# Condition rows loaded seven half products ahead, their bias fetched with them, and neighbouring weight columns read in one transfer

## The chip, the cores and the metric

The kernel runs on one core of a Trainium2 chip. The metric is the device time of one execution in microseconds; lower is better. The engines named below are TensorE (PE, matmuls), VectorE (DVE), ScalarE (ACT), GpSimd (POOL, here almost only an issuer of DMAs) and SyncE (SP, which issues most loads). Each works through its own list of instructions in order.

## The reference, cut to what matters

```python
sh1, sc1, g1, sh2, sc2, g2 = split(silu(c) @ ada_w + ada_b, 6)     # c: 1 x 1024, ada_w: 1024 x 6144
h = rmsnorm(x, norm1_g) * (1 + sc1) + sh1                          # x: 1024 tokens x 1024
gate_b, gate_c, hv = split(h @ conv_w_in, 3)                       # conv_w_in: 1024 x 3072
y = (gate_b * conv3(gate_c * hv)) @ conv_w_out                     # three taps along 64-token rows
x = x + g1 * y
gate, up = split((rmsnorm(x, norm2_g) * (1 + sc2) + sh2) @ ffn_w_in, 2)
x = x + g2 * ((silu(gate) * up) @ ffn_w_out)                       # d_ff 2816
out = rmsnorm(x, final_g)
```

All is float32. Of the six condition rows, `sh1` and `sc1` are needed at once; `g1`, `sh2`, `sc2` and `g2` only after the first projection. `ada_w` is 24 MB: 4 MB for each of the six rows.

## The kernel before

Every float32 matmul is made as three matmuls of a high and a low part (`TERMS`: high by high, high by low, low by high). The parts come from a split: ACT casts the raw tile to the high part (L83), DVE subtracts to get the low part (L74). The projections further use a two-by-two block scheme with seven products in place of eight (`P1` to `P7`), whose operands are sums of blocks (`AS1` to `AS4` of the activations, `BP3` to `BP7` of the weights, made by DVE subtractions of `wr` tiles at L74).

The part of the program that is changed is the late part of the first projection. Its 24 column tiles of 128 are named by (i, j): i is the tile in a quarter, j is 0, 1 or 2 for `gate_b`, `gate_c` and `hv`. Twelve of them, each with its partner in the other half, are handled in `PAIRS`, two at a time: `Mix(n)` takes `PAIRS[2n:2n+2]`, for n from 0 to 5. A mix needs five products (`PLAN`: P5, P6, P7, P4, P3), and for each of them a left and a right column tile a = 0, 1. Five products times two tiles times six mixes make 60 *half products*; each is 12 matmuls of 128x128 by 128x512 (`product`, L453), into the same PSUM tile `m{n}_{a}` that is emptied and filled anew between products (`after`): after P5, ACT copies it to `z5` (L464) and puts the kept product `p1` in it (L465); after P6, DVE adds to `p1` (L77); after P7, DVE adds `z5` (L77) and multiplies; after P4, the tile is put in its place (ACT copy L490 for j = 2, DVE product L80 else) and refilled with `p1` (L481); after P3, it is put in its place and, for j = 0, the finished gated tile `cv` goes by a POOL DMA to the DRAM tensor `vd` (L486).

A loop `for t in range(62)` sets the order: slot t first issues what was booked with `loads(t, ...)`, then one weight sum, the split for the next product, what was booked with `also(t, ...)`, and then half product t with its `after`. `order5` interleaves mixes 0 and 1 in slots 0 to 19; from slot 20 each mix has ten slots. All this stands under `in_order(SP, DVE, ACT, PE)`, so the four engines execute in the order in which the code is written, whatever is ready. POOL is outside of that list.

Between these products, three of the late condition rows (`g1`, `sh2` and `sc2`, 12 MB of `ada_w`) are computed, nearly without TensorE: `AdaRow` objects `rows[0..5]`, named `ada{j0}_{d0}` (`ada2_0` and `ada2_512` for `g1`; `ada3_0`, `ada3_256`, `ada3_512`, `ada3_768` for `sh2` and `sc2`; 2 MB each). For each, four loads (`load`, L200, SP) bring 512 KB each; ACT scales each by the condition (`scale`, two instructions at L205, and after the second and fourth a POOL DMA that accumulates one tile onto another, L207); DVE adds the rest and splits it (`sums`, L77, and L83/L74); two PE matmuls with ones sum over partitions (L237); then `row` fetches the bias by a POOL DMA (L240), adds it on DVE (L77, tile `ada_b`) for `g1`, or copies on ACT (L243) for the others, and writes the row out (L244). The table `ROWS` holds, for each row, the slots of its loads, of its scales and of its sums; `row` comes two slots after the last sum.

The last slots also load and split `conv_w_out` (`output_load` L937, `output_split`, tiles `wor`, `woh`, `wol`). After the loop come the output products `y` (L1005), whose other operand is `vd` read back (`vl_t`, L993) and split (`vh_t` on ACT, L83).

Of the kernel before, what the change touches and what calls it, by code (L numbers as in the profile page):

```python
# [15 lines left out]
P = 128  # L16
H = 512
# [7 lines left out]
def trunk_kernel(ctx: ExitStack, tc: tile.TileContext, x, c, ada_w, ada_b, norm1_g, norm2_g,  # L25
                 conv_w_in, conv_w, conv_w_out, ffn_w_in, ffn_w_out, final_g, out):
    nc = tc.nc
    x, out = x[0], out[0]
    T, D = x.shape
    KD = D // P  # L30
    KH = KD // 2
# [6 lines left out]
    conv_w_in, conv_w_out, conv_w = conv_w_in[0], conv_w_out[0], conv_w[0]  # L38
# [16 lines left out]
    def t_wop(name, shape):  # L55
        return sb.tile(shape, F32R, name=name, tag="wop", bufs=8)
# [7 lines left out]
    def t2(name, shape=None):  # L64
        return sb.tile(shape or [P, H], F32, name=name, tag="t2", bufs=6)
# [122 lines left out]
    class AdaRow:  # L188
# [32 lines left out]
        def sums_of_rows(self):  # L221
# [7 lines left out]
                    nc.vector.scalar_tensor_tensor(acc, row, by, acc, op0=ALU.mult, op1=ALU.add)  # L229
            self.halves(acc)  # L230

        def row(self, to, bias=False):

            nj = self.nj
            ps = bank(f"{self.name}_ps")
            for i, part in enumerate(self.parts):
                nc.tensor.matmul(ps[0:1, :], lhsT=ones_r, rhs=part, start=i == 0, stop=i == 1)  # L237
            b = t2(f"{self.name}_b")
            if bias:
                nc.gpsimd.dma_start(b[0:1, :], ada_b[0:1, self.j0 * D + self.d0:self.j0 * D + self.d0 + self.w])  # L240
                add(b[0:1, :], ps[0:1, :], b[0:1, :])
            else:
                nc.scalar.copy(b[0:1, :], ps[0:1, :])  # L243
            nc.gpsimd.dma_start(to[:, :, self.d0:self.d0 + self.w], b[0:1, :].rearrange("p (j w) -> p j w", j=nj))  # L244

# [83 lines left out]

    PAIRS = [(0, 2), (0, 1), (1, 2), (1, 1), (0, 0), (2, 2), (2, 1), (1, 0), (3, 2), (3, 1), (2, 0), (3, 0)]
    EARLY = PAIRS[:7]
    place = {(i, j): 3 * j - 2 + i if j else 0 for i, j in EARLY}
    for kp in range(2):
        a_tiles("11", kp), a_tiles("12", kp)
# [2 lines left out]

    aside = dram.tile([len(PAIRS) + 2 * KH, P, H], F32, name="aside")  # L340

# [22 lines left out]
    def save_p1(pair, tile):  # L364
        nc.scalar.copy(tile, xbank[pair])
        nc.gpsimd.dma_start(aside[PAIRS.index(pair)], tile)

    def first_done(pair):

        (i, j), ps = pair, xbank.pop(pair)  # L370
        if j == 1:
            u = parts11.pop(i)
            mul(u, ps, u)
            nc.gpsimd.dma_start(aside[len(PAIRS) + i], u)
        else:
# [4 lines left out]
            else:  # L380
                nc.gpsimd.dma_start(aside[len(PAIRS) + KH + i], u)

# [30 lines left out]
    class Mixes:  # L413
# [5 lines left out]
        def __init__(self, n):  # L419
            self.n, self.pairs, self.raw, self.w, self.ps = n, PAIRS[2 * n:2 * n + 2], {}, {}, {}  # L420

        def load(self, name, tile=t_wraw):

            n = self.n
            if name == "p1":
                self.p1 = t4(f"p1_{n}", [P, 2, H])
                nc.sync.dma_start(self.p1, aside[2 * n:2 * n + 2].rearrange("a p t -> p a t"))
                return
            k0, second = (int(q) - 1 for q in name)
            self.raw[name] = tile(f"wr{name}_{n}", [P, 2, KH, P])  # L430
            for a, (i, j) in enumerate(self.pairs):
                c = j * D + (i + second * KH) * P
                nc.sync.dma_start(self.raw[name][:, a],
                                  conv_w_in[k0 * H:(k0 + 1) * H, c:c + P].rearrange("(k p) n -> p k n", p=P))

        def sum(self, pname):

# [3 lines left out]
                sub(b[o], b[x], b[y])  # L441

        def split(self, pname):
            w = self.w[pname] = [t_wop(f"B{pname}{s}_m{self.n}", [P, 2, KH, P]) for s in "hl"]
            split(*w, self.raw[self.SUMS[pname][0] if pname in self.SUMS else "22"])

        def product(self, q, a):
            (pname, aname), (i, j) = self.PLAN[q], self.pairs[a]
            if q == 0:
                self.ps[a] = bank(f"m{self.n}_{a}")  # L450
            for k in range(KH):
                for n, (wi, hi) in enumerate(TERMS):
                    nc.tensor.matmul(self.ps[a], lhsT=self.w[pname][wi][:, a, k, :],  # L453
                                     rhs=A[aname, k // 2][hi][:, k % 2, :],
                                     start=(q == 0 and k == 0 and n == 0), stop=(k == KH - 1 and n == 2),
                                     skip_group_check=q > 0)
# [205 lines left out]
    with in_order(ENG.SP, ENG.DVE, ENG.Activation, ENG.PE):  # L662
# [5 lines left out]
        more = []  # L668

        def next_loads(k):  # L670

            if k < KD:
                ada.append(Ada(k, 1))
                ada[k].load()
                ada[k].load()
                load0(k)
            elif k == KD:
                xs.extend(Tokens(TH + i) for i in range(TH))
            elif k == KD + 1:
                more.extend(First(pair) for pair in PAIRS[7:9])  # L680
                for m in more:
                    m.load(0)
            elif k == KD + 2:
                more.extend(First(pair) for pair in PAIRS[9:])
                for m in more[2:]:
                    m.load(0)
                for m in more:
                    m.load(1)
# [59 lines left out]
        sub(h_of(0, 0)[1], h0, f(h_of(0, 0)[0]))  # L748
        by_pair = [(pair, range(3)) for pair in EARLY]
        by_term = [(pair, (i,)) for i in (0, 2, 1) for pair in EARLY]  # L750
# [117 lines left out]
        rows = [AdaRow(*p) for p in pieces]  # L868
# [28 lines left out]
        def also(t, *units):  # L897
            ahead[t][1].extend(units)

        def loads(t, *units):  # L900
            ahead[t][0].extend(units)
# [10 lines left out]
        for i, at6 in enumerate((((17, 17, 22), (19, 19, 21)), ((30, 30, 32), (28, 28, 31)),  # L912
                                 ((37, 41, 42), (44, 47, 49)), ((50, 51, 52), (53, 54, 55)))):
            loads(at6[0][0] - 2, conv[i].load)
            for n in range(2):
                for k, t in enumerate(at6[n]):
                    also(t, lambda i=i, n=n, k=k: conv[i].step(n, k))

        ROWS = (((8, 9, 10, 11), (10, 11, 12, 13), (18, 20, 23, 24)),
# [5 lines left out]
        for r, (at_load, at_scale, at_sum) in enumerate(ROWS):  # L925
            for k in range(4):
                loads(at_load[k], lambda r=r, k=k: rows[r].load(t_s if k or r in (0, 3) else t4))
                also(at_scale[k], lambda r=r, k=k: rows[r].scale(k))
                also(at_sum[k], lambda r=r, k=k: rows[r].sums(k))
            if r < 5:  # L930
                also(at_sum[3] + 2, lambda r=r: rows[r].row(rows3) if rows[r].j0 == 3 else rows[r].row(g_rows[0], True))

# [7 lines left out]
        def output_split(k):  # L940
            raw, = wo[k]
            wo[k] = [t_sr(f"wo{s}_{k}", [P, D]) for s in "hl"]
            split(*wo[k], raw)

        for k in range(6):
            loads(52 + k, lambda k=k: output_load(k))
            also(57 + k * 2 // 3, lambda k=k: output_split(k))
        for k in range(6, 8):
            loads(60, lambda k=k: output_load(k))
            also(61, lambda k=k: output_split(k))  # L950
# [2 lines left out]
        for t in range(62):  # L953
# [6 lines left out]
            if t < 60:  # L960
                n, q = order5[t // 2]
# [484 lines left out]
```

## Time and profile before

| | us |
|---|---|
| median of 3 runs (lowest to highest) | 1014.91 (1014.53 to 1016.23) |
| the profiled execution's own time | 1015.26 |
| its span, first to last instruction | 1013.5 |
| PE busy | 988.1 (97%) |
| DVE busy | 716.5 (71%) |
| ACT busy | 484.5 (48%) |
| POOL busy | 101.7 (10%) |

The profile is of one execution. All stages below are in microseconds from the start of its span; the 62 slots begin at 97 us and their last product matmul starts at 276.67 us. PE is busy almost throughout, so what can be won are the few microseconds in which it stands still, and the place to look for them is the list of what PE waited for, stage by stage. Matmul durations are modelled ends: their starts, 0.227 us apart in a row of product matmuls, tell more.

### The profile page before, as it was taken

The numbers are of one execution on the slowest core, as the hardware profiler recorded it, in microseconds if no ns is written. First come the engines' busy times: TensorE is split into PE (matmuls) and PEld (weight loads), VectorE is DVE, ScalarE is ACT, GpSimd is POOL, SyncE is SP. The second block draws the span as 40 slices with busy tenths as digits, with TensorE's granted clock in tenths as the row PEclk, the third lists the DMA queues.
The fourth block names the chain that finished last, engine by engine and source line by source line (L and its number), as shares of the span: only waits on it lengthen the run. The fifth ranks groups of instructions, "written<-read, shape, count | busy, mean of one in ns | idle before, by whom it ended". The sixth has DMA issues, their size and how long they took to land.

```text
span 1013.5 us, 12324 instructions
## 1 busy us (share of the span) xinstructions
PE 988.1 (97%) x4426; PEld 809.8 (80%) x4426; DVE 716.5 (71%) x1037; ACT 484.5 (48%) x767; POOL 101.7 (10%) x183
## 2 busy tenths in 40 slices
PE   8999999989999999999999999999999999999996
PEld 6788887767778878888888888888888888888886
DVE  5767978767846689687756656656656745778885
ACT  6555676665425566333333333333334352544653
POOL 2121001110011110111101101101101110000000
PEclk9999999999999999999999999999999999999999
DMA  9997189988685232265333333333315964578533
GB/s 298 324 329 241 56 247 256 291 252 228 221 255 188 97 110 79 92 192 169 118 100 108 104 98 110 105 94 114 104 32 194 382 224 145 181 249 280 184 127 143
DMA packets 161661, 180.46 MB, mean 178 GB/s; under 512 B 8212, under 2 KB 118912, under 8 KB 161600
## 3 DMA queue, kind: packets, MB, share of 16 engines
q1 hardware_dynamic: 147920, 135.81, 43.3%
q0 software_dynamic: 12448, 40.69, 12.5%
q10 hardware_dynamic: 1232, 3.18, 0.8%
q8 instruction: 34, 0.56, 0.2%
q14 instruction: 27, 0.22, 0.1%
HBM read 135.33 MB, written 38.03 MB: 171 GB/s over the span
## 4 chain that ended last, share of the span: by engine, by line
PE 75%; DMA 8%; DVE 8%; issue 3%; ACT 3%; SPq 1%; POOL 1%; ACTq 0%; POOLq 0%; DVEq 0%
PE X_f L563 23%; PE zP L1375 20%; PE Z_f L563 12%; PE Y_f L563 6%; PE y L1005 5%; PE m L453 3%; DMA ada_w<-in_ada_w_dram 3%; PE x L403 2%; PE x L361 2%; DMA vl_t<-vd 1%; DMA wr<-in_conv_w_in_dram 1%; DMA w0r<-in_conv_w_in_dram 1%; DVE wr L74 1%; DMA vd<-cv 1%; DMA ada_b<-in_ada_b_dram 1%
## 5 line engine op out<-in xcount | busy, mean ns | idle before, releaser
L74 DVE TENSOR_TENSOR BP_f<-wr_f,BP_f 128x512 fp32r<-128x512 f32 x154 | 105.0, 688 | 60.6 <-ACT BP_f L83 58.7
L83 ACT CAST BP_f<-wr_f 128x512 fp32r<-128x512 f32 x154 | 94.2, 621 | 86.1 <-PE Z_f L563 55.8
L1375 PE MATMUL zP<-w3l_P,a3h_P 128*128 128x512 f32 (+1 forms) x319 | 121.8, 382 | 0.0
L1375 PE MATMUL zP<-w3h_P,a3l_P 128*128 128x512 f32 (+1 forms) x319 | 121.7, 382 | 0.0
L1375 PE MATMUL zP<-w3h_P,a3h_P 128*128 128x512 f32 (+1 forms) x319 | 120.4, 382 | 0.6 <-DVE bot L80 0.6
L1375 PEld LDWEIGHTS zP<-w3h_P,a3h_P 128*128 128x128 f32 x319 | 60.0, 188 | 12.5 <-DVE bot L80 0.8
L1375 PEld LDWEIGHTS zP<-w3h_P,a3l_P 128*128 128x128 f32 x319 | 60.0, 188 | 11.6
L1375 PEld LDWEIGHTS zP<-w3l_P,a3h_P 128*128 128x128 f32 x319 | 60.0, 188 | 11.5
L74 DVE TENSOR_TENSOR a3l_P<-a3l_P,a3h_P 128x1024 fp32r<-128x1024 f32 (+1 forms) x42 | 47.3, 1132 | 24.5 <-ACT a3h_P L1230 24.5
L563 PE MATMUL X_f<-A11h,BP_f 128*128 128x512 f32 x176 | 57.7, 390 | 0.0
L563 PE MATMUL X_f<-AS3h,BP_f 128*128 128x512 f32 x176 | 57.6, 389 | 0.0
L563 PE MATMUL Z_f<-AS4h,BP_f 128*128 128x512 f32 x176 | 57.6, 389 | 0.0
L563 PE MATMUL X_f<-AS2h,BP_f 128*128 128x512 f32 x176 | 57.6, 389 | 0.0
L563 PE MATMUL X_f<-A22h,BP_f 128*128 128x512 f32 x176 | 57.6, 389 | 0.0
L563 PE MATMUL Y_f<-A12h,BP_f 128*128 128x512 f32 x176 | 57.5, 389 | 0.0
L563 PE MATMUL Z_f<-AS1h,BP_f 128*128 128x512 f32 x176 | 57.4, 389 | 0.0
L1005 PE MATMUL y<-woh,vh_t 128*128 128x512 f32 x128 | 50.6, 395 | 0.9 <-ACT vh_t L83 0.9
L1005 PE MATMUL y<-woh,vl_t 128*128 128x512 f32 x128 | 50.0, 391 | 0.0
L1005 PE MATMUL y<-wol,vh_t 128*128 128x512 f32 x128 | 49.9, 390 | 0.0
L1230 ACT CAST a3h_P<-a3l_P 128x1024 fp32r<-128x1024 f32 (+1 forms) x42 | 40.7, 979 | 15.2 <-DMA a3l_P<-ad_S 9.0
L74 DVE TENSOR_TENSOR wr_f<-wr_f,wr_f 128x512 f32<-128x512 f32 x66 | 45.3, 689 | 1.5
L77 DVE TENSOR_TENSOR u_f<-Z_f,u_f 128x512 f32<-128x512 f32 x22 | 15.2, 691 | 37.5 <-ACT u_f L580 34.8
(310 smaller groups left out, 2351.4 us busy)
## 6 DMA issues: line engine op xcount, KB each, us to landing
wr_f<-in_ffn_w_in_dram SPq DMA_DIRECT2D x44, 512.0 KB, 4.0
ada_w<-in_ada_w_dram SPq DMA_DIRECT2D x64, 256.0 KB, 6.3
w_P<-in_ffn_w_out_dram SPq DMA_DIRECT2D x30, 512.0 KB, 5.4
wr<-in_conv_w_in_dram SPq DMA_DIRECT2D x48, 256.0 KB, 6.2
a3l_P<-ad_S SPq DMA_DIRECT2D x20, 512.0 KB, 6.2
ad<-a POOLq DMA_DIRECT2D x33, 256.0 KB, 2.4
ada_w<-in_ada_w_dram SPq DMA_DIRECT2D x16, 512.0 KB, 4.0
a3l_P<-ad SPq DMA_DIRECT2D x15, 512.0 KB, 4.0
```

The costliest lines, as they stand in the source:

```text
L74: return nc.vector.tensor_tensor(o, a, b, op=ALU.subtract)
L77: return nc.vector.tensor_tensor(o, a, b, op=ALU.add)
L83: nc.scalar.copy(hi, raw)
L361: nc.tensor.matmul(xbank[pair], lhsT=w0[k][wi][:, place[pair], :], rhs=h_of(k, 0)[hi], start=(k == 0 and i == 0), stop=(k == KD - 1 and i ...
L403: nc.tensor.matmul(xbank[self.pair], lhsT=self.w[wi][:, k, :], rhs=h_of(half * KH + k, 0)[hi], start=(half == 0 and k == 0 and i == 0), st ...
L453: nc.tensor.matmul(self.ps[a], lhsT=self.w[pname][wi][:, a, k, :], rhs=A[aname, k // 2][hi][:, k % 2, :], start=(q == 0 and k == 0 and n = ...
L563: mm = nc.tensor.matmul(ps, lhsT=w[:, wi, 2 * kp + kk, :], rhs=A[aname, kp][hi][:, kk, :], start=(first and kp == 0 and kk == 0 and i == 0 ...
L1005: mm = nc.tensor.matmul(ys[t][n], lhsT=vt[t][vi][:, k, :], rhs=wo[k][wi][:, n * H:(n + 1) * H], start=(k == 0 and i == 0), stop=(k == KD - ...
L1230: nc.scalar.copy(hi, f(lo))
L1375: mm = nc.tensor.matmul((zs[t] if to is None else to)[:, cols], lhsT=a[ai][:, k % 2, t * P:(t + 1) * P], rhs=w[wi][:, k % 2, cols], start= ...
```

## The change

1. `PAIRS` is put in another order so that the two tiles of mix 0 are (0,2) and (1,2), and of mix 1 (0,1) and (1,1): neighbours in `conv_w_in`. The weight tiles are now laid out with the two tiles side by side in a row, and where the two columns are neighbours (mixes 0, 1 and 5) one DMA of 512 KB with rows of 1 KB replaces two of 256 KB with rows of 512 B. That makes 12 weight loads fewer on SP's queue. Before, mix 0 held (0,2), (0,1), and mix 1 held (1,2), (1,1).
2. In `ROWS`, loads stand three to seven slots sooner, and scales one to five; a scale now stands four slots after its load (two of them five), where it stood two to five. The sums of rows 0 to 3 stay, those of rows 4 and 5 move (row 4's first one slot later and its last two sooner, row 5's all sooner by one or two).
3. The bias of the two `g1` rows is fetched by `load_bias` three slots before the last sum, five before it is added; before, it was fetched and added at the same place.
4. The splits of `conv_w_out` stand in slots 57, 58, 59, 60, 61, 61 instead of 57, 57, 58, 59, 59, 60.

```diff
+        bias = None
+        def load_bias(self):
+            self.bias = t2(f"{self.name}_b")
+            nc.gpsimd.dma_start(self.bias[0:1, :], ada_b[0:1, self.j0 * D + self.d0:self.j0 * D + self.d0 + self.w])
+            return self.bias
...
-            b = t2(f"{self.name}_b")
             if bias:
-                nc.gpsimd.dma_start(b[0:1, :], ada_b[0:1, self.j0 * D + self.d0:self.j0 * D + self.d0 + self.w])
+                b = self.bias or self.load_bias()
                 add(b[0:1, :], ps[0:1, :], b[0:1, :])
             else:
+                b = t2(f"{self.name}_b")
                 nc.scalar.copy(b[0:1, :], ps[0:1, :])
...
-    PAIRS = [(0, 2), (0, 1), (1, 2), (1, 1), (0, 0), (2, 2), (2, 1), (1, 0), (3, 2), (3, 1), (2, 0), (3, 0)]
-    EARLY = PAIRS[:7]
+    EARLY = [(0, 2), (0, 1), (1, 2), (1, 1), (0, 0), (2, 2), (2, 1)]
+    LATER = [(1, 0), (3, 2), (3, 1), (2, 0), (3, 0)]
+    PAIRS = [(0, 2), (1, 2), (0, 1), (1, 1)] + EARLY[4:] + LATER
...
-            self.raw[name] = tile(f"wr{name}_{n}", [P, 2, KH, P])
-            for a, (i, j) in enumerate(self.pairs):
-                c = j * D + (i + second * KH) * P
-                nc.sync.dma_start(self.raw[name][:, a],
-                                  conv_w_in[k0 * H:(k0 + 1) * H, c:c + P].rearrange("(k p) n -> p k n", p=P))
+            self.raw[name] = tile(f"wr{name}_{n}", [P, KH, 2 * P])
+            (c0, c1), rows = [j * D + (i + second * KH) * P for i, j in self.pairs], conv_w_in[k0 * H:(k0 + 1) * H, :]
+            for to, c, w in ((0, c0, 2 * P),) if c1 == c0 + P else ((0, c0, P), (P, c1, P)):
+                nc.sync.dma_start(self.raw[name][:, :, to:to + w],
+                                  rows[:, c:c + w].rearrange("(k p) n -> p k n", p=P))
...
-                    nc.tensor.matmul(self.ps[a], lhsT=self.w[pname][wi][:, a, k, :],
+                    nc.tensor.matmul(self.ps[a], lhsT=self.w[pname][wi][:, k, a * P:(a + 1) * P],
...
-        ROWS = (((8, 9, 10, 11), (10, 11, 12, 13), (18, 20, 23, 24)),
-                ((14, 15, 17, 18), (16, 18, 20, 22), (26, 27, 29, 33)),
-                ((22, 23, 24, 25), (24, 25, 26, 28), (34, 37, 38, 39)),
-                ((29, 30, 31, 32), (32, 33, 34, 35), (40, 43, 44, 45)),
-                ((36, 37, 38, 39), (38, 39, 40, 42), (48, 50, 53, 56)),
-                ((43, 44, 45, 46), (45, 46, 47, 48), (57, 58, 59, 60)))
+        ROWS = (((1, 2, 3, 4), (5, 6, 7, 8), (18, 20, 23, 24)),
+                ((10, 11, 12, 13), (14, 15, 16, 17), (26, 27, 29, 33)),
+                ((18, 19, 20, 21), (22, 23, 25, 26), (34, 37, 38, 39)),
+                ((26, 27, 28, 29), (30, 31, 32, 33), (40, 43, 44, 45)),
+                ((33, 34, 35, 36), (37, 38, 39, 40), (49, 50, 51, 53)),
+                ((40, 41, 42, 43), (44, 45, 46, 47), (55, 57, 57, 58)))
...
+            if rows[r].j0 == 2:
+                loads(at_sum[3] - 3, rows[r].load_bias)
...
-            also(57 + k * 2 // 3, lambda k=k: output_split(k))
+            also((57, 58, 59, 60, 61, 61)[k], lambda k=k: output_split(k))
```

What this does to the engines' lists is shown at three places. Lines of the changed kernel are seven to eleven higher for the same statement.

ACT, at the end of the first product of mix 2 (slot 20). `BP7h_m2` is the high part of mix 2's third weight sum, `cv0_1` a convolution's first tap, `z5_2_0` the copy out of the PSUM tile `m2_0`, and the next row its refill. Before:

```order
L205 ACTIVATE ada2_512_w2_1394<-ada2_512_w2_1394,cols_98 128x512 x2
L490 COPY u1_1_1133<-m1_0_1116 128x512
L83 CAST BP7h_m2_1477<-wr12_2_1275 128x1024
L512 ACTIVATE cv0_1_1481<-u0_1_1088,cols2_778 128x1024
L205 ACTIVATE ada2_512_w4_1435<-ada2_512_w4_1435,cols_98 128x512 x2
L464 COPY z5_2_0_1517<-m2_0_1504 128x512
L465 COPY m2_0_1504<-p1_2_1433 128x512
```

And with the change:

```order
L83 CAST BP6h_m2_1436<-wr11_2_1277 128x1024
L521 ACTIVATE cv0_0_1440<-u0_0_1079,cols2_778 128x1024
L205 ACTIVATE ada2_512_w6_1348<-ada2_512_w6_1348,cols_98 128x512 x2
L499 COPY u1_1_1106<-m0_1_1089 128x512
L83 CAST BP7h_m2_1480<-wr12_2_1280 128x1024
L521 ACTIVATE cv0_1_1484<-u0_1_1080,cols2_778 128x1024
L473 COPY z5_2_0_1521<-m2_0_1508 128x512
L474 COPY m2_0_1508<-p1_2_1434 128x512
```

The scales of `ada2_512` that stood around the convolution's tap and right ahead of the copy of `z5_2_0` are now all ahead of `u1_1`, and nothing but the tap stands between `BP7h_m2` and the copy.

POOL, around the bias of the row `ada2_512` (the DMA from `in_ada_b_dram`, L240 before and L236 now). Rows with L207 accumulate one tile of a condition row onto another, `vd` rows send a finished `cv` tile away, and the `g1_row` row sends the biased row. Before:

```order
L486 DMA vd_125<-cv0_0_1441 128x1024
L207 DMA ada3_0_w4_1592<-ada3_0_w6_1616 128x1024
L486 DMA vd_125<-cv0_1_1481 128x1024
L207 DMA ada3_256_w0_1712<-ada3_256_w2_1736 128x1024
L240 DMA ada2_512_b_1860<-in_ada_b_dram 1x16x32
L207 DMA ada3_256_w4_1762<-ada3_256_w6_1786 128x1024
L244 DMA g1_row_126<-ada2_512_b_1860 16x1x32
```

And with the change:

```order
L251 DMA g1_row_126<-ada2_0_b_1527 16x1x32
L495 DMA vd_125<-cv0_0_1440 128x1024
L236 DMA ada2_512_b_1737<-in_ada_b_dram 1x16x32
L495 DMA vd_125<-cv0_1_1484 128x1024
L207 DMA ada3_256_w0_1638<-ada3_256_w2_1665 128x1024
L207 DMA ada3_256_w4_1691<-ada3_256_w6_1713 128x1024
L251 DMA g1_row_126<-ada2_512_b_1737 16x1x32
```

The bias fetch stood behind the first accumulation of `ada3_256`; it now stands ahead of it, and ahead of `cv0_1` too.

DVE, at the end of the loop. `cv3_1` multiplied by `m5_1` is the last step of the last mix; `wol` rows are the low parts of `conv_w_out`, `vl_t` rows those of `vd` read back. Before:

```order
L74 TENSOR_TENSOR wol_2_2377<-wor_2_2290,woh_2_2376 128x1024
L80 TENSOR_TENSOR cv2_1_2079<-m5_0_2214,cv2_1_2079 128x512
L77 TENSOR_TENSOR ada3_768_w0_2054<-ada3_768_w0_2054 128x512
L74 TENSOR_TENSOR wol_3_2397<-wor_3_2307,woh_3_2396 128x1024
L74 TENSOR_TENSOR wol_4_2401<-wor_4_2324,woh_4_2400 128x1024
L80 TENSOR_TENSOR cv3_1_2274<-m5_1_2235,cv3_1_2274 128x512
L74 TENSOR_TENSOR ada3_768_l_2424<-ada3_768_w0_2054,ada3_768_h_2423 128x512
L74 TENSOR_TENSOR wol_5_2428<-wor_5_2344,woh_5_2427 128x1024
L74 TENSOR_TENSOR wol_6_2432<-wor_6_2419,woh_6_2431 128x1024
L74 TENSOR_TENSOR wol_7_2436<-wor_7_2421,woh_7_2435 128x1024
```

And with the change:

```order
L74 TENSOR_TENSOR wol_1_2366<-wor_1_2257,woh_1_2365 128x1024
L80 TENSOR_TENSOR cv2_1_2073<-m5_0_2202,cv2_1_2073 128x512
L74 TENSOR_TENSOR wol_2_2385<-wor_2_2282,woh_2_2384 128x1024
L80 TENSOR_TENSOR cv3_1_2263<-m5_1_2224,cv3_1_2263 128x512
L74 TENSOR_TENSOR wol_3_2408<-wor_3_2299,woh_3_2407 128x1024
L74 TENSOR_TENSOR wol_4_2412<-wor_4_2323,woh_4_2411 128x1024
L74 TENSOR_TENSOR wol_5_2416<-wor_5_2339,woh_5_2415 128x1024
L74 TENSOR_TENSOR wol_6_2420<-wor_6_2403,woh_6_2419 128x1024
L74 TENSOR_TENSOR wol_7_2424<-wor_7_2405,woh_7_2423 128x1024
L74 TENSOR_TENSOR vl_t2_2506<-vl_t2_2506,vh_t2_2505 128x512
```

The product of `cv3_1` stood behind `wol_3` and `wol_4` and now stands ahead of both; the low part `vl_t2` went behind all `wol` rows, and row `ada3_768` has left this stretch.

More of the change, by code (lines that the diff above doesn't have):

```diff
@@ L443, in split @@
         def split(self, pname):
-            w = self.w[pname] = [t_wop(f"B{pname}{s}_m{self.n}", [P, 2, KH, P]) for s in "hl"]
+            w = self.w[pname] = [t_wop(f"B{pname}{s}_m{self.n}", [P, KH, 2 * P]) for s in "hl"]
             split(*w, self.raw[self.SUMS[pname][0] if pname in self.SUMS else "22"])
@@ L679, in next_loads @@
             elif k == KD + 1:
-                more.extend(First(pair) for pair in PAIRS[7:9])
+                more.extend(First(pair) for pair in LATER[:2])
                 for m in more:
@@ L683, in next_loads @@
             elif k == KD + 2:
-                more.extend(First(pair) for pair in PAIRS[9:])
+                more.extend(First(pair) for pair in LATER[2:])
                 for m in more[2:]:
```

## The prediction

> **What bounds the kernel now.** I read the page's totals first, then the busy times by stage, then what PE waited for in the stage that the change touches, and then the timeline of each engine around each of those waits.
>
> ```profile
> span 1013.5 us, 12324 instructions
> PE 988.1 (97%) x4426; PEld 809.8 (80%) x4426; DVE 716.5 (71%) x1037; ACT 484.5 (48%) x767; POOL 101.7 (10%) x183
> 97.00:300.00 203.00, 193.20 (x831) 154.42 (x830) 157.80 (x176) 118.62 (x163) 20.73 (x31) 0.99 0.80 231
> 300.00:1013.00 713.00, 703.96 (x3164) 582.93 (x3162) 492.55 (x728) 306.23 (x493) 60.88 (x106) 1.00 0.45 147
> ```
>
> The second pair of rows counts PE first: busy time and, in brackets, instructions. PE is the bound. From 97 to 300 us, which is the 62 slots and the first output products, it is idle for 203.00 - 193.20 = 9.8 us, as much as in the 713 us behind (9.0). What it waits for there:
>
> ```profile
> PE m L453 <- DVE z L77: 3.7, 1, 3.7
> PE m L453 <- ACT m L481: 2.8, 2, 1.6
> PE m L453 <- ACT m L465: 1.3, 1, 1.3
> PE m L453 <- DVE p L77: 1.1, 2, 0.8
> PE y L1005 <- ACT vh_t L83: 0.9, 1, 0.9
> ```
>
> These five groups, seven waits, are the whole 9.8 us. They cost more than their idle time. In a row of product matmuls starts are 0.227 us apart, and after a wait the first few come slower:
>
> ```profile
> 201.82 0.39 PE L453 MATMUL m<-A22l,BP4h_m 128*128 128x512 f32 x1
> 202.05 0.39 PE L453 MATMUL m<-A22h,BP4l_m 128*128 128x512 f32 x1
> 206.09 0.79 PE L453 MATMUL m<-A22h,BP4h_m 128*128 128x512 f32 x1 [3.66 <-DVE z L77]
> 206.69 0.63 PE L453 MATMUL m<-A22l,BP4h_m 128*128 128x512 f32 x1
> 209.49 0.40 PE L453 MATMUL m<-A22h,BP4l_m 128*128 128x512 f32 x1
> ```
>
> From 206.09 to 209.49 nine starts take 3.40 us where 9 x 0.227 = 2.04 would do. So this wait (C below) costs 3.66 idle and 1.4 to 1.6 of slowed matmuls. I summed, for all 831 PE rows, what each start-to-start distance over 0.33 us has above 0.227: 14.2 us in all, of which 5.4 are C. That is the most that the change can win here; the profiled execution's own time is 1015.26, and the median of the runs lies 0.35 below it. A difference of 0.2%, 2 us, is about what a measurement of this kernel can tell.
>
> **The seven waits, and what the change does to each.** I give idle time, and with the slow first starts in brackets.
>
> A, 1.31 (1.8), slot 22: P6 of mix 2 waits for the ACT copy that refills `m2_0`.
>
> ```profile
> 156.30 1.32 ACT L205 ACTIVATE ada_w<-ada_w,cols 128x512 f32<-128x512 f32 x2
> 157.53 0.56 ACT L464 COPY z<-m 128x512 f32<-128x512 f32 x1
> 158.12 0.59 ACT L465 COPY m<-p 128x512 f32<-128x512 f32 x1
> 158.76 0.50 PE L453 MATMUL m<-AS2h,BP6h_m 128*128 128x512 f32 x1 [1.31 <-ACT m L465]
> ```
>
> The two scales of `ada2_512` stand ahead of the copies. In the new ACT list they are earlier, and the P5 tile that the copies need was done a whole half product (12 x 0.227 = 2.7 us) before PE stood still. The copies, 1.2 us for the pair, then wait for PE alone. A goes.
>
> C, 3.66 (5.4), slot 37: the second tile of P4 of mix 3 needs a DVE sum that stands behind the bias sum.
>
> ```profile
> 196.63 0.80 POOL L240 DMA_DIRECT2D ada_b<-in_ada_b_dram  x1
> 204.76 0.68 DVE L77 TENSOR_TENSOR ada_b<-ada_ps,ada_b 1x512 f32<-1x512 f32 x1 [3.53 <-DMA ada_b<-in_ada_b_dram]
> 205.37 0.67 DVE L77 TENSOR_TENSOR z<-m,z 128x512 f32<-128x512 f32 x1
> DMA to landing us min/median/max: 1.7/5.2/9.2
> ```
>
> The bias DMA was issued at 196.63 and landed 8.06 us later; 9.2 is the longest of the four. With the change it is booked five slots ahead, 5 x 12 x 0.227 = 13.6 us before the add, and its place in POOL's list is behind a `vd` DMA whose `cv0_0` is ready at slot 26. So it lands at least 4 us before it is wanted, and C loses its 5.4. What is late next is DVE itself: its list up to that sum is done 0 to 0.3 us after PE wants it. Two slots on, at 39, the refill of `m3_1` stands in a chain of a multiplication, two copies, a cast and two DVE passes, which C had hidden; with durations from their rows I get 0.45 late. Cost of both: 0.6.
>
> E, 1.62 (1.9), slot 49, and F, 1.22 (1.5), slot 59: refills of `m4_1` and `m5_1`.
>
> ```profile
> 235.73 1.34 ACT L205 ACTIVATE ada_w<-ada_w,cols 128x512 f32<-128x512 f32 x2 [2.46 <-DMA ada_w<-in_ada_w_dram]
> 243.00 0.69 DVE L80 TENSOR_TENSOR u<-m,u 128x512 f32<-128x512 f32 x1
> 243.72 0.59 ACT L481 COPY m<-p 128x512 f32<-128x512 f32 x1 [1.36 <-DVE u L80]
> 272.87 0.62 ACT L83 CAST vh_t<-vl_t 128x512 fp32r<-128x512 f32 x1 [3.16 <-DMA vl_t<-vd]
> 273.39 0.58 ACT L481 COPY m<-p 128x512 f32<-128x512 f32 x1
> ```
>
> E begins with ACT idle for 2.46 us until a load of `ada3_768` lands, which pushes the cast of `BP6h` and all behind it. That load is now three slots (8 us) earlier and its scale one slot. F's refill stands behind the cast of `vh_t2`, which waits for a `vd` read; now the refill is ahead of it, and one `wol` pass (2.36 for two, 1.2 for one) leaves the DVE list ahead of it. I take 0.3 each for what DVE's queue still costs (0 if its passes run at the rows' times from here, 1.9 and 1.5 if nothing moves).
>
> B, 0.78 (1.05), and D, 0.31 (0.6), slots 24 and 44: P7 waits for the DVE add to `p1`.
>
> ```profile
> 161.78 2.44 DVE L516 SCALAR_TENSOR_TENSOR cv<-u,cols,cv 128x1008 f32<-128x1008 f32 x2
> 164.25 0.69 DVE L80 TENSOR_TENSOR cv<-cv,gate 128x512 f32<-128x512 f32 x1
> 164.86 0.68 DVE L77 TENSOR_TENSOR p<-m,z 128x512 f32<-128x512 f32 x1
> 227.46 0.68 DVE L77 TENSOR_TENSOR p<-m,z 128x512 f32<-128x512 f32 x1
> ```
>
> Here DVE's queue is simply long: two convolution taps (2.44) and two more passes stand ahead of the add at 164.86. The amount of DVE work stays. For B the copies of A come sooner and start the queue sooner: 0.3 left, between 0 and 1.05. D began with a scale that waited for its load; I put it at 0.
>
> G, 0.90 (1.45), at 294: `y` waits for the last `vd` read back.
>
> ```profile
> 276.60 0.69 DVE L80 TENSOR_TENSOR cv<-m,cv 128x512 f32<-128x512 f32 x1
> 277.80 2.35 DVE L74 TENSOR_TENSOR wol<-wor,woh 128x1024 fp32r<-128x1024 f32 x2
> 280.07 0.69 DVE L80 TENSOR_TENSOR cv<-m,cv 128x512 f32<-128x512 f32 x1
> 281.06 0.53 POOL L486 DMA_DIRECT2D vd<-cv  x1 [1.20 <-DVE cv L80]
> 293.66 0.62 ACT L83 CAST vh_t<-vl_t 128x512 fp32r<-128x512 f32 x1 [9.58 <-DMA vl_t<-vd]
> 294.33 0.50 PE L1005 MATMUL y<-woh,vh_t 128*128 128x512 f32 x1 [0.90 <-ACT vh_t L83]
> ```
>
> The last product matmul starts at 276.67, yet the multiplication runs only at 280.07, behind two `wol` passes of 1.2 us; then POOL's DMA, the read and the cast take 280.07 to 294.28. With the change two passes of `wol` and one of `ada3_768` are behind the multiplication and `g1` is behind the `vd` DMA on POOL: the chain starts 1.2 us or more sooner. Two `y` matmuls that PE ran ahead of the last product now come after it, so PE also arrives 0.45 later. G goes, with 0.1 left.
>
> **What the change adds.** Scales now run earlier and their tiles are reused earlier. The tightest place I find is slot 34: in ACT's new list the convolution's tap on `cv1_1` reuses the buffer of an `ada3_0` tile, so it waits for the accumulating DMA of that row, and the cast for `BP7` of mix 3 stands behind it, then three DVE passes and the add to `p1` that PE wants.
>
> ```profile
> L207 POOL DMA_DIRECT2D ada_w<-ada_w x12: 851/875/914, 131.9 to 245.9; - x12
> DMA to landing us min/median/max: 4.6/7.9/9.6
> ```
>
> The scale before it runs at about 170.2 in old times; with 7.9 us to landing the tap starts at 178.4, and the add is done about 0.6 us after PE wants it. With 4.6 the wait is 0; with 9.6 it is 2.3. I take 1.0, since this sum follows some fifteen passes by their mean durations and since a late DVE pass already ends three of the seven waits. Slots 28 and 54 come out at 0 to 0.2 and 0 to 0.5: 0.35 for both.
>
> Twelve weight loads fewer are twelve issues of about 0.4 us fewer on SP. By the loop's bookings a load stands one to three products ahead of its use, so this is worth nothing on the path; nor do I charge the 1 KB rows anything, since DVE needs both column tiles in one pass and waits for the later of the two loads anyway. If a merged load landed as late as the slower of two does now, nothing changes. The first row's four loads move up to slots 1 to 4 and its scales to 5 to 8, where DVE is full:
>
> ```profile
> 110.00:130.00 20.00, 20.00 (x90) 16.57 (x89) 19.97 (x22) 9.81 (x11) 0.00 (x0) 1.00 0.29 79
> ```
>
> The third number is DVE: 19.97 of 20 us busy. PE does not wait there now, so what is late by less than its lead costs nothing. ACT waits for DVE between its casts, the scales fit into those gaps, and the casts that come about 1.4 us later (one scale pair) are ones that DVE takes up later than that: 0 for the early row, with up to 1.5 if one of them is not. The last split slots cost nothing but what G counts. Behind 300 us nothing moves.
>
> **Sum.** Left of the 14.2: A 0, B 0.3, C and slot 39 0.75, D 0, E 0.3, F 0.3, G 0.1, slot 34 1.0, slots 28 and 54 0.35, small slow starts that belong to none of them 0.5: 3.6. The saving is 10.6; 1015.26 - 10.6 = 1004.7, and with the 0.35 between this execution and the median, 1004.3.
>
> **Rivals.** (1) The queues take the waits back. DVE and ACT do the same work in the same time, so B, D, E and F return in full at neighbouring slots (5.0) and slot 34 costs 2.0. For it: DVE at 19.97 of 20, and three of the seven waits end on a late DVE pass. Against it: E and F begin with ACT waiting for DMAs that are now early. The saving is then A 1.8, C 5.4 less 0.75, G 1.45, less 2.0: 5.9, or 1009.0. (2) All new waits stay out: the saving is 14.2 - 0.5 = 13.7, or 1001.2. For it: each new wait is at most 0.5 us by my passes but slot 34's. (3) The bias comes no sooner because POOL's list holds it behind something that waits: C stays, 10.6 - 4.65 = 6.0, or 1009.0. Against it: the `vd` DMA ahead of it needs only `cv0_0`. (4) C's slowed matmuls were of the profiled execution only. The runs shown differ by 1.7 us, about the size of what the slowed starts cost, so some executions may not have had them. C then had 3.9 to give (3.66 and 0.2), the saving is 9.1, and with it 1005.8. Against it: the profiled execution, which had them, lies in the middle of the three. [...] (5) Slower: the tap on `cv1_1` at slot 34. Each microsecond that the accumulating DMA lands later goes to PE in full, since ACT, DVE and PE stand in order behind it. It decides when that wait passes 1.0 + 10.6 = 11.6 us, that is, when the accumulation lands at about 189 in old times; over 2 us more, and it is slower beyond doubt: 1017 at 13.6. For it: the tile's accumulation is issued behind another on POOL, which waits for its own loads and scales first. Against it: 9.6 us is the longest landing seen, and the table issues these loads four and five slots earlier than before.
>
> **How the numbers follow.** My forecast 0.48; rival 1 0.22; rival 2 0.13; rival 4 0.07; rival 3 0.03; slower by over 0.2%, rival 5 above all, 0.04; a mix in which so much returns that it is within 0.2% 0.03. The range goes from rival 2, 1001.2, to a little over rivals 1 and 3, 1009.5; outside of it lie the last two cases and the edges of rivals 1 and 2, some 0.15. The forecast's own bounds, with each term at its ends, are about 1002.5 to 1006.5. Faster is 0.93, within 0.2% 0.03, slower 0.04.
>
> **What would show it.** In the list of PE's waits the 3.7 behind DVE `z` is gone, or under 0.5, and no matmul after it is slowed; the wait for the refill at L465 is gone; the two at L481 are under 0.5 each; `y` no longer waits for `vh_t`. The bias DMA is issued some 14 us before its add. PE's idle time from 97 to 300 is 2 to 4 us in place of 9.8. A wait of over 1.5 us at slot 34, with ACT behind a POOL DMA, would show that I took the accumulation too lightly; waits behind `p` or `z` passes of DVE at many slots would show rival 1; a lasting wait before 157 would mean that the early row disturbs the first two mixes.

## The result and the profile after

The changed kernel takes 1002.46 us (median of 4, 1000.76 to 1002.73) against 1014.81 (median of 4, one execution more than in the table of before): the ratio is 0.987, 95% interval 0.986 to 0.989. The profiled execution took 1002.73. Its page totals, and the busy times of two stretches, as before with PE first:

```profile
span 1000.9 us, 12305 instructions
PE 983.8 (98%) x4426; PEld 808.9 (81%) x4426; DVE 716.3 (72%) x1037; ACT 484.2 (48%) x767; POOL 101.0 (10%) x183
20.00:40.00 20.00, 18.23 (x83) 14.48 (x83) 15.88 (x39) 7.86 (x11) 0.11 (x1) 0.91 1.17 308
98.00:288.00 190.00, 189.96 (x835) 154.81 (x834) 158.46 (x178) 118.73 (x163) 20.71 (x31) 1.00 0.84 244
```

From 98 to 288 us, which holds the 62 slots and the first `y` products, PE is busy 189.96 of 190.00 us. In place of seven waits with 9.8 us the list of PE's waits is empty for that stage. Counted in matmul starts (what lies above 0.227 us between starts more than 0.33 apart), the stage loses 0.58 us where it lost 14.2. The third row shows the granted clock, third from the end of the row: 0.91 from 20 to 40 us, where it was 1.00 before. There some of the gain went back in this execution, 0.9 us until the loop began; the second profile of the same kernel has starts 0.23 us apart at 33 us (below).

C, slot 37, in the timelines of POOL, DVE and PE:

```profile
174.05 0.50 POOL L236 DMA_DIRECT2D ada_b<-in_ada_b_dram  x1
196.99 0.67 DVE L77 TENSOR_TENSOR ada_b<-ada_ps,ada_b 1x512 f32<-1x512 f32 x1
197.59 0.67 DVE L77 TENSOR_TENSOR z<-m,z 128x512 f32<-128x512 f32 x1
200.00 0.39 PE L462 MATMUL m<-A22h,BP4h_m 128*128 128x512 f32 x1
```

The bias DMA goes out at 174.05, 23 us ahead of the add, where the forecast said some 14: POOL is outside the list that `in_order` holds and runs ahead of the slots (PE begins slot 30, for which this DMA is booked, at 180.46). The add at 196.99 waits for nothing. The sum that PE wants is done at 198.26, 1.7 us before PE takes it up at 200.00. A and G:

```profile
155.67 0.59 ACT L473 COPY z<-m 128x512 f32<-128x512 f32 x1 [2.27 <-PE m L462]
156.29 0.59 ACT L474 COPY m<-p 128x512 f32<-128x512 f32 x1
265.24 1.22 DVE L74 TENSOR_TENSOR wol<-wor,woh 128x1024 fp32r<-128x1024 f32 x1
266.38 0.68 DVE L80 TENSOR_TENSOR cv<-m,cv 128x512 f32<-128x512 f32 x1
267.36 0.53 POOL L495 DMA_DIRECT2D vd<-cv  x1 [1.20 <-DVE cv L80]
278.51 0.62 ACT L83 CAST vh_t<-vl_t 128x512 fp32r<-128x512 f32 x1 [3.83 <-DMA vl_t<-vd]
```

The copy into `z5` now waits for PE, and the refill is done at 156.88, 1.3 us before P6 starts at 158.19. At the end of the loop one `wol` pass instead of two stands between the last product and the multiplication, and the cast of `vh_t` is done before PE comes to it.

### The profile page after: what moved, and what is told of

It is laid out like the page before. It is cut to its first block, busy times and chain, and to the rows that moved or that the text cites. A ratio compares the mean times of both kernels' runs of the same rounds, so it can differ in the third digit from the quotient of the medians.

```text
span 1000.9 us, 12305 instructions
## 1 busy us (share of the span) xinstructions
PE 983.8 (98%) x4426; PEld 808.9 (81%) x4426; DVE 716.3 (72%) x1037; ACT 484.2 (48%) x767; POOL 101.0 (10%) x183
## 2 busy tenths in 40 slices
DMA packets 155325, 180.46 MB, mean 180 GB/s; under 512 B 8020, under 2 KB 112576, under 8 KB 155264
## 4 chain that ended last, share of the span: by engine, by line
PE 91%; DMA 3%; DVE 2%; SPq 2%; ACT 1%; issue 1%; POOL 0%; POOLq 0%; ACTq 0%; DVEq 0%
PE X_f L572 23%; PE zP L1386 20%; PE m L462 16%; PE Z_f L572 12%; PE y L1016 7%; PE Y_f L572 6%; PE x L412 3%; PE x L370 2%; SPq L154 1%; DMA ada_w<-in_ada_w_dram 1%; PE x1T L989 1%; SPq L354 1%; DMA wr_f<-in_ffn_w_in_dram 1%; DMA x<-in_x_dram 0%; DMA vl_t<-vd 0%
```

## The experiments

Two theories went in. P: each of the seven waits hangs on one instruction in a wrong place, so that parts of the change act alone. Q: the gain comes of fewer and earlier loads as a whole. "Stage loss" is the sum over starts, as above, for 205 us from the first product of the loop, in the profiled execution alone. Each ratio is to executions of the kernel before that were taken beside it; their medians lie between 1014.81 and 1015.78.

| kernel | median us | ratio to before (95%) | stage loss us |
|---|---|---|---|
| before | 1014.81 | 1 | 14.23 |
| changed | 1002.46 | 0.9872 (0.9855 to 0.9889) | 0.58 |
| bias alone, on before | 1011.28 | 0.9967 (0.9956 to 0.9978) | 10.01 |
| changed, late bias | 1004.14 | 0.9902 (0.9886 to 0.9917) | 2.32 |
| changed, old table of rows | 1007.91 | 0.9936 (0.9922 to 0.9950) | 8.05 |
| changed, two loads for each merged one | 1001.38 | 0.9867 (0.9850 to 0.9885) | 1.02 |
| changed, old pairs and two loads | 1001.60 | 0.9868 (0.9850 to 0.9886) | 1.41 |
| changed, old end | 1004.50 | 0.9898 (0.9882 to 0.9914) | 3.59 |
| changed, early loads but old scale slots | 1009.07 | 0.9941 (0.9925 to 0.9956) | 9.02 |
| the same, `ada3_0` with new scale slots | 1003.14 | 0.9875 (0.9857 to 0.9893) | 2.01 |
| changed, one ACT tap five times | 1004.57 | 0.9887 (0.9869 to 0.9906) | 2.87 |
| changed, terms reordered at 30 us | 1002.56 | 0.9876 (0.9859 to 0.9894) | 0.59 |
| changed, once more | 1001.98 | 0.9867 (0.9846 to 0.9888) | 0.58 |

**The bias alone.** The kernel before with this edit, and the method `load_bias` that it calls:

```diff
+            if rows[r].j0 == 2:
+                loads(at_sum[3] - 3, rows[r].load_bias)
```

> The kernel before with the early bias fetch alone. Theory P (each of the seven waits hangs on one instruction that stood in a wrong place): wait C (3.66 idle, 5.4 with slowed matmuls) goes, its successor at slot 39 costs 0.4 to 1, the other six waits stay with 6.1 us idle; time 4.5 to 5 below the kernel before, about 1010. Theory Q (the gain comes from the whole, fewer and earlier loads, which relieve the DMA queues and with them DVE and ACT): the bias lands early but DVE is late anyway, C shrinks only in part, 1012 or more.

```profile
PE m L460 <- ACT m L488: 4.1, 3, 1.6
PE m L460 <- DVE p L77: 1.1, 2, 0.8
PE y L1014 <- ACT vh_t L83: 1.0, 1, 1.0
PE m L460 <- ACT m L472: 0.9, 1, 0.9
```

C is gone from PE's waits, the other six are there (the group of refills at L488 now has three). The third is C's successor, the refill of `m3_1` at slot 39: 1.05 us idle, where 0.4 to 1 was expected. The loss falls by 4.2 us, the median by 3.9, from 1015.13. The time lies between the two expectations; the waits are those of P.

**The changed kernel with the late bias,** the two lines above taken out of it.

> The changed kernel with the bias fetched where it is added, as before. Theory P: in POOL's list the fetch now stands behind the second accumulation of ada3_256 at 192, so it lands at 196 to 201 where DVE takes it up at 197; PE waits 0 to 2.5 us at slot 37, time 1002.5 to 1005. If the bias cost what it cost before the change, a wait of 3.7 with slowed matmuls would come back: 1007 to 1008. Theory Q: with the queues relieved the fetch lands in 2 to 4 us, no wait, 1002.5.

```profile
PE m L462 <- ACT m L490: 1.0, 1, 1.0
192.70 0.84 POOL L236 DMA_DIRECT2D ada_b<-in_ada_b_dram  x1
198.90 0.68 DVE L77 TENSOR_TENSOR ada_b<-ada_ps,ada_b 1x512 f32<-1x512 f32 x1 [1.86 <-DMA ada_b<-in_ada_b_dram]
```

The bias lands 1.86 us late, and of that PE pays 0.12 at slot 37, 0.07 at 38 and 1.05 at 39 (the row above; waits that short are not listed). So the early bias is worth 4.2 us on the kernel before and 1.7 here. With the early rows the late fetch is issued 3.9 us sooner (192.70 against 196.63) while PE is 2.3 us further along, and it lands after 6.1 us in place of 8.06, in both kernels within 0.5 us of the accumulating DMA issued just ahead of it. The parts are not independent in this pair.

**The old table of rows in the changed kernel.**

```diff
-        ROWS = (((1, 2, 3, 4), (5, 6, 7, 8), (18, 20, 23, 24)),
+        ROWS = (((8, 9, 10, 11), (10, 11, 12, 13), (18, 20, 23, 24)),
...
```

> The changed kernel with the old table of rows (loads, scales and sums), but early bias, merged loads and new slots for the last splits. Theory P: A, B, D and E return (5.3 us with slow starts), F and G in part since the sums of the last row stand at 57 to 60 again (1 to 2), C stays away: 1008 to 1009.5. Theory Q: most of the gain stays with the merged loads, under 1006.

```profile
PE m L462 <- ACT m L490: 2.2, 2, 1.1
PE m L462 <- ACT m L474: 2.1, 1, 2.1
PE m L462 <- DVE p L77: 1.2, 2, 0.8
PE m L462 <- DVE z L77: 0.5, 1, 0.5
136.95 1.34 ACT L205 ACTIVATE ada_w<-ada_w,cols 128x512 f32<-128x512 f32 x2 [2.56 <-DMA ada_w<-in_ada_w_dram]
```

By the new table the loads of the first row stand seven slots sooner, those of the others three to five; an old scale stood two to four slots after its load. A (L474, 2.1), B and D (`p`, 1.2 in two) and E (1.1, one of the two refills at L490) are back. So is C's successor at slot 39 (1.05, the other), and DVE is 0.5 us late at slot 37 (`z`), though the bias is early; neither was expected. F and G stay away, although the old sums of the last row are back too. 7.5 us of loss are back, the most of the four parts of the change. The last row shows where A begins: ACT waits 2.56 us for a load of `ada2_0`, 20 us ahead of the wait on PE. The run with early loads and old scale slots (below) has the same ACT list here without that wait. Counted from the start of the loop, ACT is 2.6 us later than there at this row and still 2.7 us later at the copy into `z5`.

**Two loads for each merged one, and the old pairs too.**

```diff
-            for to, c, w in ((0, c0, 2 * P),) if c1 == c0 + P else ((0, c0, P), (P, c1, P)):
+            for to, c, w in ((0, c0, P), (P, c1, P)):
```

> The changed kernel with two loads of 256 KB in place of each merged one; order of pairs and all else as changed. Theory P: no wait comes back, within 0.3 us of the changed kernel, 1002.5. Theory Q: twelve more issues on SP and rows of 512 B make weights late, 1 us or more slower, with waits of ACT and DVE on wr tiles.

> The changed kernel with the old order of pairs and two loads everywhere; rows, bias and last slots as changed. Theory P: no wait comes back that costs over 0.3 us, 1002.5 within 0.5. Theory Q: 1 us or more slower.

Stage losses of 1.02 and 1.41 against 0.58: one wait on `z` of 0.16 us in the first, and waits of 0.15 on `p` and 0.13 on `z` in the second. The medians are 1001.38 and 1001.60, not above the changed kernel's 1001.98 to 1002.46. Twelve DMAs fewer and rows of 1 KB for 512 B are worth less than these runs can tell. Of Q, the half that speaks of fewer loads has nothing left for it.

**The old end.**

```diff
-            also((57, 58, 59, 60, 61, 61)[k], lambda k=k: output_split(k))
+            also(57 + k * 2 // 3, lambda k=k: output_split(k))
```

and the old sums of rows 4 and 5.

> The changed kernel with the old slots at the end: splits of conv_w_out at 57, 57, 58, 59, 59, 60 and the old sums of rows 4 and 5; loads and scales as changed. Theory P: F and G return, 1.5 and 1.45 with their slow starts, 1004.5 to 1005.5, with PE waits for the refill at slot 59 and for vh_t. Rival: F and G came only from the waits ahead of them (E pushed them), so they stay away: under 1003.2.

```profile
PE m L462 <- ACT m L490: 1.5, 1, 1.5
PE y L1016 <- ACT vh_t L83: 0.7, 1, 0.7
263.58 0.62 ACT L83 CAST vh_t<-vl_t 128x512 fp32r<-128x512 f32 x1 [3.30 <-DMA vl_t<-vd]
264.10 0.58 ACT L490 COPY m<-p 128x512 f32<-128x512 f32 x1
```

F and G return, as F was in the kernel before: the refill at 264.10 right behind a cast that waited 3.30 us for `vd`. Together 3.0 us of loss, 2 to 2.5 in the medians. With the old rows but the new end they stayed away, so the old sums alone do not bring them back: it takes the old slots of the splits. Whether those slots would do it with the new sums, no run shows.

**Early loads, old scale slots.**

```diff
-                ((18, 19, 20, 21), (22, 23, 25, 26), (34, 37, 38, 39)),
+                ((18, 19, 20, 21), (24, 25, 26, 28), (34, 37, 38, 39)),
...
```

and the old scale slots in the five other rows.

> The changed kernel with the early loads but each scale in its old slot. If A and E came from where the scale stands in ACT's list, A returns at 1.3 idle and with it B (0.8), and E in part: 1004.5 to 1006. If they came from scales that waited for their loads (1.62 us at 147 and 2.46 at 235 in the kernel before), early loads alone remove them: under 1003.2, with A under 0.4.

```profile
PE m L462 <- ACT m L474: 4.1, 1, 4.1
PE m L462 <- DVE p L77: 0.9, 2, 0.7
180.44 0.89 POOL L207 DMA_DIRECT2D ada_w<-ada_w  x1 [4.82 <-ACT ada_w L205]
155.05 1.32 ACT L205 ACTIVATE ada_w<-ada_w,cols 128x512 f32<-128x512 f32 x2
156.28 0.56 ACT L473 COPY z<-m 128x512 f32<-128x512 f32 x1
188.62 1.15 ACT L521 ACTIVATE cv<-u,cols 128x1024 f32<-128x1024 f32 x1 [6.61 <-DMA ada_w<-ada_w]
190.92 0.80 PE L462 MATMUL m<-AS2h,BP6h_m 128*128 128x512 f32 x1 [4.09 <-ACT m L474]
191.51 0.63 PE L462 MATMUL m<-AS2l,BP6h_m 128*128 128x512 f32 x1
196.63 0.49 PE L462 MATMUL m<-AS2l,BP6h_m 128*128 128x512 f32 x1
```

Neither expectation had this. A and E are gone: the scales stand right ahead of the copy of `z5` again (155.05 and 156.28), and PE finds the refill done 0.5 us early. So A and E came from scales that waited for loads. B is there (0.7 at slot 24). But a new wait of 4.1 us stands at slot 32: the tap on `cv1_0` is to write into a buffer that the accumulating DMA of `ada3_0` still reads, waits 6.61 us for it (issued 180.44, landed 188.54), and the refill of `m3_0` is behind it on ACT. After the wait the matmuls start 0.43 apart for 5.7 us. The prediction had named the tap on `cv1_1`; here that one starts at 177.76, ahead of the DMA, and the next tap inherits the delay.

**The same with new scale slots for `ada3_0` alone.**

> The kernel with early loads and old scale slots, except that row ada3_0 has its new scale slots. If the wait of 4.1 us at slot 32 there came from the tap on cv1_0, whose buffer waited for ada3_0's late accumulating DMA (180.44 to 188.54), it is gone together with its slowed matmuls, and what is left is the wait on p in slot 24 (0.7) and slot 54 (0.2): 1003 to 1004. If the old scales crowd ACT in general, half of the wait stays: 1005 or more.

The 4.1 us wait and the slowed matmuls are gone. In the list of PE's waits only the row for `p` is left, the same as above (0.7 at slot 24, 0.2 at slot 54), and the time is 1003.14 us. That is the first expectation, and it shows that one late accumulation cost 7 us of stage loss.

**A late ACT by itself.**

```diff
-                nc.scalar.mul(self.cv[n], mixed[i, n], cw[1])
+                for _ in range(5 if (i, n) == (1, 1) else 1):
+                    nc.scalar.mul(self.cv[n], mixed[i, n], cw[1])
```

> The price of lateness on ACT just ahead of slot 34, by itself: the changed kernel with the first tap of cv1_1 executed five times in place of once (same result each time), 4.2 to 4.6 us more on ACT ahead of the cast for BP7 of mix 3. If each microsecond there goes to PE in full beyond a lead of about 1.1 us, as the prediction had it, PE loses 3.1 us or more, 1005.5 or more. If idle stretches of ACT and DVE behind it give back some (DVE waits 2.0 us at 183.6, ACT 2.8 us at 169.9 and 1.8 at 178.9 in the profile of the changed kernel), the loss is about 1.5, half at the refill of m3_0 in slot 32 and half at p in slot 34: 1004.

```profile
PE m L462 <- ACT m L474: 1.4, 2, 1.0
PE m L462 <- ACT m L490: 0.4, 1, 0.4
174.70 5.89 ACT L522 ACTIVATE cv<-u,cols 128x1024 f32<-128x1024 f32 x5
180.63 1.27 DVE L526 SCALAR_TENSOR_TENSOR cv<-u,cols,cv 128x1008 f32<-128x1008 f32 x1 [4.50 <-ACT cv L522]
190.72 0.68 DVE L77 TENSOR_TENSOR p<-m,z 128x512 f32<-128x512 f32 x1
```

The five taps take 5.89 us where one took 1.15, DVE idles 4.50 us for them, and PE loses 2.3 us of stage loss, between the two expectations. So idle stretches did give back about half. (The expectation put one of them, on ACT at 169.9, at 2.8 us; in the trace it is 3.3.) The place was right for slot 32 alone: 1.0 there and 0.35 at slot 33, both refills on ACT, and 0.4 at slot 39. There is none at slot 34, where the add on `p` is done at 191.40, in time.

**A faster version, tried.** `for n, (pair, terms) in enumerate(by_term if k < 3 else by_pair)` in the first projection; a second line of the edit keeps the sum of the next condition row behind as many matmuls as before.

> A try at a faster version: the changed kernel, and in the first part of the program (row block 2 of the first projection, at 29 us) the terms that need the low part of the activations come last, as they do for row block 1, so that PE has 14 matmuls to do while DVE makes that part. The wait of 0.92 us at 30 (1.2 with its slow start) goes: 1001.3. If the slowed matmuls that follow that wait in the profiled execution of the changed kernel (9 starts at 0.43, 1.7 us) come from it, they go too in every execution: about 1000, with a mean clock of 0.998 throughout. If they come by chance, independent of that wait, some executions keep 0.996.

```profile
33.95 0.38 PE L179 MATMUL ada_ps<-ones,ada_acc 128*128 128x1 f32 x2 [1.29 <-DVE ada_acc L77]
```

The wait for `A11l` is gone, and 1.29 us of waiting for `ada_acc` came in its place 3 us later, since the same DVE list makes both. 1002.56 us: no gain. The mean clock of its four executions is 0.996, not 0.998: in its profile the slowed matmuls stand at 17 to 20 us instead of 33 (granted clock 0.72 from 15 to 20 us, 0.94 from 20 to 25 and 1.00 from 30 to 40), so they do not hang on that wait alone. None of these runs beats the changed kernel by more than they can tell.

**The changed kernel once more.**

> The changed kernel once more, beside executions of the kernel before on the same chip. If the slowed matmuls follow a long wait by chance, the kernel before spreads over 4 us or more from run to run and the changed kernel, which has no long wait but the one at 30 us, over 2.5 at most; median about 1002.

1001.98 us, 1001.33 to 1002.82. The seven executions of the kernel before on that chip go from 1013.94 to 1018.26. Both spreads are as expected. The PE timeline at the same instructions, of the first profile of the changed kernel and then of this one:

```profile
33.03 0.60 PE L370 MATMUL x<-A11h,w0h 128*128 128x512 f32 x1
33.43 0.63 PE L370 MATMUL x<-A11l,w0h 128*128 128x512 f32 x1
36.42 0.51 PE L370 MATMUL x<-A11h,w0l 128*128 128x512 f32 x1
```

```profile
33.45 0.48 PE L370 MATMUL x<-A11h,w0h 128*128 128x512 f32 x1
33.77 0.39 PE L370 MATMUL x<-A11l,w0h 128*128 128x512 f32 x1
35.38 0.40 PE L370 MATMUL x<-A11h,w0l 128*128 128x512 f32 x1
```

From the first to the last of these rows, eight steps, one takes 3.39 us and the other 1.93; the waits ahead of them are the same (0.92 for `A11l`, three smaller).

## Why the prediction was right, step by step

1004.3 us was forecast, with 1001.2 to 1009.5, and 1002.46 came. The saving in the stage was 13.65 us where the sum said 10.6; so in this stage rival 2, with 13.7, is what happened. Of the 3.6 us that the sum left over, 0.58 came, 0.30 at slot 39 and 0.27 at slot 49. That the time is nearer to the forecast than the stage is chance: the 0.9 us lost ahead of the loop in the profiled execution hide part of the difference.

- C: right in mechanism, and its successor at slot 39 was right in place. (Between 206.09 and 209.49 lie eight steps, not nine, so the slowed matmuls cost 1.6; and the working ends at 0.6 for both places, while the sum takes 0.75.) DVE's list was said to end 0 to 0.3 late at slot 37; it has 1.7 us to spare. The refill at slot 39 was said to be 0.45 late and costs 0.04 idle, 0.3 with slow starts. Three other runs show it at 1.05 idle: the early bias alone, the late bias, and the old table of rows.
- A: gone, but the step's reason failed. It was put down to the two scales ahead of `z5`. With the scales there and the loads early, PE does not wait; with the old table ACT waits 2.56 us for a load, and A is back. In the kernel before, ACT waits for loads 1.04 us at 134 and 1.62 us at 147, both ahead of A. The scales passed on a lateness that began at a load.
- E: right, and for the reason given (the load of `ada3_768`). B and D: gone with slack of 0.8 and 1.2 us; B was given 0.3. B is the one that needs early scales too: it is there at 0.7 in both runs with early loads and old scale slots.
- F and G: right; they came back with the old slots of the splits and the old sums, and not with the old sums alone. F has 0.16 us of slack, G's cast is 2 us or more ahead.
- Merged loads at nothing: right, by two runs.
- Slot 34, the largest term left (1.0) and the slower rival: the term was mis-sized. Its working began with 7.9 us from issue to landing of the accumulating DMA, the median of the kernel before. Measured:

```profile
170.18 0.86 POOL L207 DMA_DIRECT2D ada_w<-ada_w  x1 [5.95 <-ACT ada_w L205]
176.36 1.15 ACT L521 ACTIVATE cv<-u,cols 128x1024 f32<-128x1024 f32 x1
185.62 1.22 DVE L74 TENSOR_TENSOR BP4l_m<-wr,BP4h_m 128x1024 fp32r<-128x1024 f32 x1 [2.00 <-ACT BP4h_m L83]
189.85 0.69 DVE L77 TENSOR_TENSOR p<-m,z 128x512 f32<-128x512 f32 x1
191.34 0.39 PE L462 MATMUL m<-AS3h,BP7h_m 128*128 128x512 f32 x1
DMA to landing us min/median/max: 4.6/6.0/9.6
DMA to landing us min/median/max: 4.7/8.3/9.5
```

The DMA landed at 176.16, 6.0 us after its issue, just before ACT came to the tap; DVE then has an idle gap of 2.00 us, which the forecast's passes had not, and `p` is done 0.8 us before PE. The last two rows are the accumulating DMAs of the changed kernel and of the one with old rows: the median landing falls from 8.3 to 6.0 by the table of rows alone (6.0 and 6.1 without merged loads). With early loads and old scale slots it is 8.2, so it goes with the slots of the scales, which issue these DMAs, and not with the loads. The durations of DMAs were taken over from a schedule that the edit itself dissolved. The mechanism is real all the same: at slot 32, with a landing of 8.1 us, it made the longest wait of all the experiments, 4.1 us and 2.9 of slowed matmuls for 6.6 us on ACT. That not each microsecond on ACT goes to PE, the run with five taps shows: 2.3 us for 4.7.
- "Behind 300 us nothing moves": right, 2.8 us of lost starts before and after. Nothing was said of the time ahead of 97 us, and there the profiled execution lost some: the loop begins at 98.33 in place of 97.45. In the second profile of the changed kernel it begins at 97.22.
- Rival 4, slowed matmuls that come in some executions only: shown at another place than C. Of the nine profiles of the first nine rows of the table, which have the same code at 33 us, five (the changed kernel, the old table, two loads, the old end, old scale slots) have the slow stretch there: granted clock 0.78 to 0.84 from 30 to 35 us and 0.81 to 0.88 from 35 to 40, which is about 1.7 us lost in each. Three of the other four (the bias alone, the late bias, the old pairs) have 0.66 to 0.68 from 15 to 20 us instead, about as much, and the kernel before has 1.00 in both places. So the stretch moves more than it comes and goes. The second profile of the changed kernel has starts 0.23 us apart at 33 us, and its mean clock, 0.996, is that of the first. For C the record says this much: the kernel before has one profile, but its executions were granted mean clocks from 0.992 to 0.999. A stretch like C's (granted clock 0.50 for 3.41 us, from 205.84 us) costs 0.0017 of that, so the execution at 0.999, 1013.22 us, cannot have had it. Whether the others had theirs behind C, no run shows. These executions spread over 6 us (1012.37 to 1018.61); the changed kernel's eight have clocks from 0.996 to 0.998 and spread over 2.1.

## What to carry to other kernels

When several engines run in written order, look for the first engine that waited for a DMA, here 20 us (A, with the old table) and 7 us (E, in the kernel before) ahead of where the bound engine stops; the instruction right ahead of the stop may only pass the delay on. A landing time in a trace belongs to the traffic of that schedule (the median of the accumulating DMAs was 8.3 us with the old table and 6.0 with the new one): when an edit moves the transfers, take a range for it, and ask for each buffer that is reused which DMA must have finished. Loads issued earlier can bring nothing if what is made of them keeps a late slot, since the next user of the buffer then inherits the delay (6.61 us on ACT at slot 32): early loads with old scale slots ran at 1009.07, the old table at 1007.91.

## What the runs showed of the hardware

Waits of PE of up to 2.1 us inside the loop left the mean granted clock at 1.00 (98 to 302 us of the run with the old table of rows). After those of 1.31 and 1.62 us in the kernel before, the first step between starts was 0.34 us and the next ones 0.23. With the wait of 3.66 us (C) came a granted clock of 0.50, from 205.84 us for 3.41 us: the first step was 0.60, and the next ones were 0.43 until 209.25, 3.2 us after the first start. With the one of 4.09 us (early loads, old scale slots) it was 0.76 in the mean from 186 to 200 us, with steps of 0.43 until 5.7 us after the first start. At 33 us the same 0.43 came in the first profile of the changed kernel after waits of 0.26, 0.92 and 0.11 us, with no long wait just ahead of it: from 28.62 to 33.03 us PE was idle for 1.3 us in 4.4. The granted clock there varies between profiles with the same code: it is 0.78 to 0.84 from 30 to 35 us in the five named above and 1.00 in the other four. One of these four, the kernel before, has waits of 0.26 and 0.91 us there; the second profile of the changed kernel has its 0.92 too, and steps of 0.23 at 33 us. What brought the slow stretch there in five profiles, and not in the others, no run shows.
